# A hybrid attention and convolution block on one core: TensorE's order written by hand, and a value projection with weights stationary

## The chip, the cores and the metric

The kernel runs on one core of a Trainium2 chip. The metric is the device time of one execution in microseconds (us); the median over several executions is given. One more execution was recorded by the hardware profiler, and every row below is from that one. TensorE (PE in the rows, PEld for its weight loads) multiplies, VectorE (DVE), ScalarE (ACT) and GpSimd (POOL) do the rest, and SyncE (SP) issues nearly all transfers.

## The reference

The input has 2048 rows of 1024 numbers, ahead of which stand 16 meta tokens. All is in f32.

```python
proj = x @ w_in                        # q, k, v, z_a, u_c, g_c, z_c, gate_a, gate_c
# attention, 16 heads of 64, keys before the query only:
#   A[t,s] = sigmoid(z_ts) * prod_{s<j<t} (1 - sigmoid(z_tj))
o   = stick_breaking_attention(heads(q), heads(k), heads(v))
y_a = (o * silu(z_a)) @ w_attn_out
u   = u_c * sigmoid(g_c)
c   = silu(layer_norm(causal_depthwise_conv(u, dw_w, dw_b)))      # 31 taps
y_c = (c * silu(z_c)) @ w_conv_out
h   = sigmoid(gate_a) * y_a + sigmoid(gate_c) * y_c
out = layer_norm(alpha * x + h @ w_out)
```

## The kernel before

The sequence is worked in two halves of 1024 rows. Each half has a phase A (`phase_a`: projections, attention, convolution) and a phase B (`phase_b`: the convolution's layer norm and both output branches); `phase_c` makes the output. The sums are held to f32 by splitting each operand into a high and a low part, so that a projection chunk is 24 matmuls (`mm3`, L153 to L155: high by high, low by high, high by low, for 8 slices of the 1024 inputs). Chunks are 512 columns wide, or 352, 352 and 336 where the 16 meta columns ride along (k and the convolution's u and g in the first half). Weights are fetched by `split_w`: in the first half as raw f32, whose high part ScalarE copies (L136) and whose low part GpSimd subtracts (L137); both are kept in DRAM for the second half. There are two buffers for each.

Phase A goes over 8 pairs of heads. Attention of a pair is a walk over blocks of 256 queries (m) and, for each, over blocks of 256 keys (j) from the diagonal down to 0; I call one such (m, j) a tick. There are 10 ticks in a pair of the first half and 26 in one of the second, 288 in all, of which 64 are on the diagonal and 64 are low (j = 0; they carry the meta tokens). A tick is: 8 score matmuls (L382), the sigmoid (ScalarE, L385 and L388), a scan along the keys (VectorE, L404), 8 transposes of the scanned tile into two banks of two (`aT`, L416), their copies to SBUF (L420 to L423) and the weighing (L435): for each of two blocks of 128 keys and each of two heads one matmul of 256 columns against 64 columns of `dv`, the differences of v along the keys. A record of the profile is one pass; an f32 matmul leaves two, so that the four weighings of a tick are eight records. Low ticks add 4 narrow transposes (L440), a copy and 2 weighings with the meta keys (L445).

v is projected for two pairs at once with x stationary (`proj_v`, L277 to L279, 256 columns wide), written to DRAM (`v_d`) and read twice, shifted by a row, so that VectorE can take the differences (`load_v`, L348 and L350; `vd` is the one for the diagonal). The convolution's 31 taps (L479, L482) run on VectorE at low priority, two pieces of 512 columns a tap. Gates (`gates`) are projections that nothing in phase A needs; some are made between the ticks, the others in phase B (`between`), while the convolution's norm (`conv_norm`: L538 to L572 on VectorE, ScalarE and GpSimd, with two column sums on TensorE, L542 and L553) is worked. The order of every engine's instructions, TensorE's too, is made by a scheduler from priorities (`tc.high_priority`, `background`) and its own notion of durations.

Of the kernel before, what the change touches and what calls it, by code (L numbers as in the profile page):

```python
# [12 lines left out]
F32 = mybir.dt.float32  # L13
# [6 lines left out]
P = 128  # L20
# [5 lines left out]
HD = 64  # L26
# [13 lines left out]
def tile_stickbreak_hybrid(ctx: ExitStack, tc: tile.TileContext, t, out: bass.AP):  # L40
# [15 lines left out]
    v_d = dram.tile([1 + META + SEQ, D], F32, name="v_d")  # L56
# [14 lines left out]
    tail = const.tile([P, KC, 32], F32, name="tail")[:, :, 0:TAPS - 1]  # L71

# [53 lines left out]
    def split_w(key, src, shape=(KC, P), pool=None, bufs=2):  # L126
# [10 lines left out]
        nc.gpsimd.tensor_tensor(wl, raw, wh.bitcast(F32), ALU.subtract)  # L137
# [11 lines left out]
    def mm3(ps, w, xh, xl, c0, n, wk=lambda a, k: a[:, k, :]):  # L149
        wh, wl = w  # L150
        for k in range(KC):
            xhk, xlk = xh[:, k, c0:c0 + n], xl[:, k, c0:c0 + n]
            nc.tensor.matmul(ps, wk(wh, k), xhk, start=(k == 0), stop=False)  # L153
            nc.tensor.matmul(ps, wk(wh, k), xlk, start=False, stop=False)  # L154
            nc.tensor.matmul(ps, wk(wl, k), xhk, start=False, stop=(k == KC - 1))  # L155
# [18 lines left out]
    def alloc_x():  # L174
        xh = xp.tile([P, KC, XW], F32R, tag="xh", name="xh")
        xl = xp.tile([P, KC, XW], F32R, tag="xl", name="xl")
        return xh, xl
# [66 lines left out]
    def phase_a(hf, xh, xl, gate_items, order):  # L244
# [7 lines left out]
        with tc.tile_pool(name=f"pa{hf}", bufs=1) as pa:  # L252
            d1 = pa.tile([P, FW], F32, name="d1")
            nc.gpsimd.memset(d1, 0.0)
            if hf == 0:
                nc.sync.dma_start(out=v_d[0:1, :], in_=d1[0:1, 0:D])
            vms = [pa.tile([P, P], F32, name=f"vm{i}") for i in range(2)]
            ams = [pa.tile([P, 512], F32, name=f"am{i}") for i in range(2 - hf)]
            for x in vms + ams:
                nc.gpsimd.memset(x, 0.0)  # L260

            own = [slice(h * HD, (h + 1) * HD) for h in range(2)]
            oth = own[::-1]

            def proj_v(g):
                wv = w_in[:, :, 2 * D + g * 256:2 * D + (g + 1) * 256]
                w0 = split_w(("v", g, 0), wv[:, 0:4, :], (4, 256))
                w1 = split_w(("v", g, 1), wv[:, 4:8, :], (4, 256))
                tiles = [(i * P, P, META + hf * HALF + i * P) for i in range(8)]
                if hf == 0:  # L270
                    tiles.insert(0, (HALF, META, 0))
                for (c0, rows_, pos) in tiles:
                    ps = bank("mm", 2)[0:rows_, 0:256]
                    for k in range(KC):
                        wh, wl = (w0, w1)[k // 4]
                        a, b = xh[:, k, c0:c0 + rows_], xl[:, k, c0:c0 + rows_]
# [3 lines left out]
                    vs = pa.tile([P, 256], F32, tag="vs", name="vs", bufs=3 - hf)  # L280
                    nc.scalar.copy(vs[0:rows_], ps)
                    nc.sync.dma_start(out=v_d[1 + pos:1 + pos + rows_, g * 256:(g + 1) * 256], in_=vs[0:rows_])

            def proj_k(p):
                w = w_chunk(1, p)
                ka = [pa.tile([P, 32 + HALF], F32R, tag=f"ka{h}", name=f"ka{h}", bufs=2 - hf)[:, KM:] for h in range(2)]
                ks = ka
                if hf == 1:
                    ks = [pa.tile([P, HALF], F32R, tag=f"kb{h}", name=f"kb{h}", bufs=2) for h in range(2)]
# [422 lines left out]
```

## Time and profile before

| | |
|---|---|
| median of 3 runs | 3440.3 us (3435.89 to 3443.79) |
| profiled execution | 3442.93 us, span of its instructions 3441.1 us |
| busy: PE, PEld, DVE, ACT, POOL | 3303.5, 2602.1, 2159.5, 1150.9, 591.5 us |
| first score, last weighing of the first half | 171 and 1123 us |
| first score, last weighing of the second half | 1565 and 2970 us |

A busy time is the sum over an engine's instructions; a matmul's own length is longer than the distance from its start to the next one's, because matmuls overlap. What a matmul costs its engine is therefore read as the distance between two starts in the timeline.

### The profile page before, as it was taken

Reading aid. Unit: us, or ns where it says so; the run is one execution under the profiler, and the core shown is the slowest. Engines: PE = TensorE matmul, PEld = TensorE weight load, DVE = VectorE, ACT = ScalarE, POOL = GpSimd, SP = SyncE. Lnnn points to the kernel's source line nnn. Section 1 sums busy time; section 2 is a strip of 40 time slices with the busy share of each in tenths; the row PEclk is TensorE's granted clock in tenths of the full one; section 3 lists DMA queues with packets and bytes.
Section 4 is the critical chain, followed back from the end, with each engine's and each line's share of the span. In section 5 each row is a group of like instructions: output and inputs, shape, how many; then the busy total and the mean of one; then the engine's idle time right before and its main releaser. Section 6 shows DMA issues by size and latency. Waiting matters only on the chain.

```text
span 3441.1 us, 48095 instructions
## 1 busy us (share of the span) xinstructions
PE 3303.5 (96%) x18657; PEld 2602.1 (76%) x18657; DVE 2159.5 (63%) x2843; ACT 1150.9 (33%) x2284; POOL 591.5 (17%) x651
## 2 busy tenths in 40 slices
PE   7999999999999898999999999999999999999999
PEld 6987877877877676787777777777777777778777
DVE  6158578568569688216757685778567875364266
ACT  4243333333333243103443344334433434331100
POOL 2121312312312445100010001000100010122000
PEclk9999999999999998999999999999999999999999
DMA  8422522522523679762222222232212221567763
GB/s 291 148 98 96 187 99 100 190 92 106 186 93 119 220 265 320 284 203 75 73 72 76 101 72 72 65 100 70 87 59 94 77 83 67 167 232 249 249 205 104
DMA packets 302214, 476.86 MB, mean 139 GB/s; under 512 B 19354, under 2 KB 190962, under 8 KB 301986
## 3 DMA queue, kind: packets, MB, share of 16 engines
q1 hardware_dynamic: 299682, 465.26, 39.8%
q0 software_dynamic: 2304, 8.52, 0.8%
q8 instruction: 147, 2.41, 0.3%
q14 instruction: 81, 0.66, 0.1%
HBM read 297.35 MB, written 176.36 MB: 138 GB/s over the span
## 4 chain that ended last, share of the span: by engine, by line
PE 61%; DVE 6%; DMA 3%; issue 2%; POOL 1%; ACT 0%; SPq 0%; POOLq 0%; DVEq 0%; ACTq 0%
PE ps_o L435 9%; PE ps_mm L155 8%; PE ps_mm L153 8%; PE ps_mm L154 8%; PE ps_aT L416 7%; PE ps_z L382 6%; PE ps_mm L599 2%; PE ps_mm L597 2%; PE ps_mm L598 2%; DVE acc L482 2%; DVE f L404 1%; PE ps_mm L279 1%; PE ps_mm L278 1%; PE ps_mm L277 1%; DMA wl<-kept_in 1%
## 5 line engine op out<-in xcount | busy, mean ns | idle before, releaser
L153 PE MATMUL ps_mm<-xh,wh 128*128 128x512 f32 (+3 forms) x2336 | 872.0, 373 | 44.7 <-DVE ka L297 14.8
L404 DVE TENSOR_TENSOR_SCAN f<-f,d 128x1028 f32<-128x1028 f32 (+1 forms) x288 | 670.4, 2328 | 372.9 <-POOL f L389 159.8
L155 PE MATMUL ps_mm<-xh,wl 128*128 128x512 f32 (+3 forms) x2336 | 870.3, 373 | 13.8 <-POOL wl L137 12.4
L154 PE MATMUL ps_mm<-xl,wh 128*128 128x512 f32 (+3 forms) x2336 | 870.3, 373 | 0.0
L482 DVE SCALAR_TENSOR_TENSOR acc<-u,dww,acc 128x512 f32<-128x512 f32 x960 | 725.5, 797 | 6.6
L153 PEld LDWEIGHTS ps_mm<-xh,wh 128*128 128x128 f32 x2336 | 446.7, 191 | 121.7 <-issue 23.2
L155 PEld LDWEIGHTS ps_mm<-xh,wl 128*128 128x128 f32 x2336 | 445.1, 191 | 84.0 <-POOL wl L137 13.6
L154 PEld LDWEIGHTS ps_mm<-xl,wh 128*128 128x128 f32 x2336 | 446.4, 191 | 62.9 <-issue 2.0
L423 ACT COPY at<-ps_aT 128x512 f32<-128x512 f32 x448 | 260.3, 589 | 686.1 <-PE ps_aT L416 674.9
L435 PE MATMUL ps_o<-at,vp 128*64 128x256 f32 (+1 forms) x2048 | 408.2, 383 | 0.0
L416 PE MATMUL ps_aT<-ident,f 128*128 128x128 f32 x2176 | 349.9, 284 | 17.1 <-DVE f L404 16.9
L416 PEld LDWEIGHTS ps_aT<-ident,f 128*128 128x128 f32 x2176 | 237.3, 141 | 170.4 <-issue 147.0
L137 POOL TENSOR_TENSOR wl<-raw,wh 128x1024 fp32r<-128x1024 f32 x88 | 255.6, 2907 | 419.0 <-ACT wh L136 401.0
L382 PE MATMUL ps_z<-ka,q 128*128 128x256 f32 (+1 forms) x1664 | 290.2, 297 | 0.0
L388 ACT ACTIVATE f<-ps_z 128x512 f32<-128x512 f32 x448 | 253.1, 603 | 110.8 <-PE ps_z L382 101.4
L435 PEld LDWEIGHTS ps_o<-at,vp 128*64 128x64 f32 x2048 | 164.9, 136 | 138.2 <-issue 74.1
L389 POOL MEMSET f<- 128x4 f32 x288 | 30.2, 106 | 1371.5 <-ACT f L388 904.7
L382 PEld LDWEIGHTS ps_z<-ka,q 128*128 128x128 f32 x1664 | 232.5, 190 | 6.4 <-issue 2.4
L597 PE MATMUL ps_mm<-ah,wh 128*128 128x512 f32 x512 | 204.5, 400 | 8.6 <-DMA wh<-kept_w_attn_out 2.9
L598 PE MATMUL ps_mm<-al,wh 128*128 128x512 f32 x512 | 203.8, 398 | 7.3 <-DVE al L585 7.2
L599 PE MATMUL ps_mm<-ah,wl 128*128 128x512 f32 x512 | 205.0, 400 | 4.5 <-DMA wl<-kept_w_conv_out 2.9
L277 PE MATMUL ps_mm<-wh,xh 128*128 128x256 f32 (+1 forms) x544 | 156.6, 288 | 1.8 <-DMA wh<-kept_v 1.6
(147 smaller groups left out, 3653.5 us busy)
## 6 DMA issues: line engine op xcount, KB each, us to landing
wh<-kept_in SPq DMA_DIRECT2D x80, 512.0 KB, 3.6
wl<-kept_in SPq DMA_DIRECT2D x80, 512.0 KB, 4.4
raw<-w_in SPq DMA_DIRECT2D x72, 512.0 KB, 4.8
kept_in<-wh SPq DMA_DIRECT2D x64, 512.0 KB, 2.6
kept_in<-wl SPq DMA_DIRECT2D x64, 512.0 KB, 3.1
vp<-v_d SPq DMA_DIRECT2D x24, 512.0 KB, 4.2
vc<-v_d SPq DMA_DIRECT2D x24, 512.0 KB, 5.7
wh<-kept_w_conv_out SPq DMA_DIRECT2D x24, 512.0 KB, 3.6
```

The source lines that it names most:

```text
L153: nc.tensor.matmul(ps, wk(wh, k), xhk, start=(k == 0), stop=False)
L154: nc.tensor.matmul(ps, wk(wh, k), xlk, start=False, stop=False)
L155: nc.tensor.matmul(ps, wk(wl, k), xhk, start=False, stop=(k == KC - 1))
L382: nc.tensor.matmul(z[:, z0:z0 + nk], qs[h][s][:, tk], kp[h][:, ks0:ks0 + nk], start=(s == 0), stop=(s == 1))
L404: nc.vector.tensor_tensor_scan(ff, ff, dd, 0.0, ALU.mult, ALU.add)
L416: nc.tensor.transpose(tp[:, (2 * blk + q) * P:(2 * blk + q + 1) * P], f[:, 2 * h + q, c:c + P], ident)
L423: nc.scalar.copy(a, tp)
L435: nc.tensor.matmul(o_ps[hs, c:c + n], v[:, b8, hs], aT[h][:, a0 + c:a0 + c + n], start=(diag and blk == 0 and i == 0), stop=False)
L482: nc.vector.scalar_tensor_tensor(a, u[:, x + k:x + k + w], dww[:, i, k:k + 1], a, ALU.mult, ALU.add)
L597: nc.tensor.matmul(ps, wh[:, k, :], hi[k], start=(k == 0), stop=False)
L598: nc.tensor.matmul(ps, wh[:, k, :], lo[k], start=False, stop=False)
L599: nc.tensor.matmul(ps, wl[:, k, :], hi[k], start=False, stop=(k == KC - 1))
```

## The change

TensorE's order within phase A is no longer the scheduler's (`tc.manual_schedule`): the code's order holds. Each tick is the transposes of tick i, the scores of tick i + 2, at least 3000 columns of projection matmuls (`fill`), the weighing of tick i in one piece, and then the rest of the tick's share of projections. Projections are `Job`s in a written list; a job loads its own weights and those of the next one. v becomes such a job (`job_v`, weights stationary, 352, 352 and 336 or 512 columns wide): it leaves v with the keys along the columns, VectorE subtracts neighbouring columns (`dT`), and a `Turn` transposes the result, 8 blocks and in the first half one for the meta keys. `load_v`, its transfers and `vd` go; the last v of each block of queries is added when the output is taken (`og`). The meta part of a low tick has one transpose instead of four, and 4 narrow weighings in the same piece as the others. The low part of the weights is subtracted on VectorE (L139). In phase A there are 15 gates in each half instead of 8, so that phase B has 3 and 7 left to put between instead of 10 and 14. The convolutions of the first half run one pair earlier.

```diff
         raw = wp.tile([P, *shape], F32, tag="raw", name="raw")
         nc.sync.dma_start(out=raw, in_=src)
         nc.scalar.copy(wh, raw)
-        nc.gpsimd.tensor_tensor(wl, raw, wh.bitcast(F32), ALU.subtract)
+        nc.vector.tensor_tensor(wl, raw, wh.bitcast(F32), ALU.subtract)
...
-    def mm3(ps, w, xh, xl, c0, n, wk=lambda a, k: a[:, k, :]):
+    def mm3_steps(ps, w, xh, xl, c0, n):
...
         for k in range(KC):
             xhk, xlk = xh[:, k, c0:c0 + n], xl[:, k, c0:c0 + n]
-            nc.tensor.matmul(ps, wk(wh, k), xhk, start=(k == 0), stop=False)
-            nc.tensor.matmul(ps, wk(wh, k), xlk, start=False, stop=False)
...
+            nc.tensor.matmul(ps, wh[:, k, :], xhk, start=(k == 0), stop=False)
+            nc.tensor.matmul(ps, wh[:, k, :], xlk, start=False, stop=False)
+            nc.tensor.matmul(ps, wl[:, k, :], xhk, start=False, stop=(k == KC - 1))
+            yield 3 * n
...
+        with tc.tile_pool(name=f"pa{hf}", bufs=1) as pa, tc.manual_schedule(engines={mybir.EngineType.PE}):
...
-            def proj_v(g):
-                wv = w_in[:, :, 2 * D + g * 256:2 * D + (g + 1) * 256]
-                w0 = split_w(("v", g, 0), wv[:, 0:4, :], (4, 256))
...
-                        nc.tensor.matmul(ps, a, wh[:, k % 4, :], start=(k == 0), stop=False)
-                        nc.tensor.matmul(ps, b, wh[:, k % 4, :], start=False, stop=False)
-                        nc.tensor.matmul(ps, a, wl[:, k % 4, :], start=False, stop=(k == KC - 1))
...
+                def steps(self):
+                    st = self.begin() if self.begin else None
+                    for (c, n, parts) in self.chunks:
+                        ps = bank("mm", 2)[:, 0:n]
+                        for cost in mm3_steps(ps, self.w, xh, xl, c, n):
+                            yield cost
+                        self.evac(st, ps, c, n, parts)
...
+                def steps(self):
+                    dT = pairs[self.p]["dT"]
+                    dv = pa.tile([P, 8, P], F32, tag="dv1", name="dv1", bufs=2 - hf)
+                    for e in range(2):
+                        tp = bank("mm", 2)
+                        for b in range(4):
+                            c = VO + (4 * e + b) * P
+                            nc.tensor.transpose(tp[:, b * P:(b + 1) * P], dT[:, c:c + P], ident)
+                        yield 4 * 240
+                        nc.scalar.copy(dv[:, 4 * e:4 * e + 4, :], tp.rearrange("p (b c) -> p b c", c=P))
+                    pairs[self.p]["dv"] = [dv]
+                    if hf == 0:
+                        nc.sync.dma_start(out=dv_d[self.p], in_=dv)
+                        tp = bank("mm", 2)
+                        nc.tensor.transpose(tp[0:META, 0:P], dT[:, VO - META:VO], ident)
+                        yield 240
+                        vm = vms[self.p % 2]
...
...
+                def evac(vT, ps, c, n, parts):
+                    for (p0, l, d0) in parts:
...
+                    dT = pa.tile([P, VO + HALF], F32, tag="dT", name="dT", bufs=1)
+                    a = VO - off
+                    nc.vector.tensor_tensor(dT[:, a:], vT[:, a - 1:VO + HALF - 1], vT[:, a:], ALU.subtract)
+                    pairs[p]["dT"], pairs[p]["vL"] = dT, vL
+                return Job(2, p, kchunks, begin, evac)
...
-                    nc.vector.tensor_tensor(prev, prev, cur_, ALU.subtract)
-                    if e == hf:
-                        nc.vector.scalar_tensor_tensor(cur_, cur_, ident[:, P - 1:P], prev, ALU.mult, ALU.add)
-                        vd = cur_
...
+            def turn_meta(fm):
+                tp = bank("aT", 2)
+                nc.tensor.transpose(tp[:, 0:P], fm, ident)
+                a = pa.tile([P, P], F32, tag="am", name="am", bufs=2)
+                nc.scalar.copy(a, tp[:, 0:P])
+                return a
...
+            def weigh(p, i, aT, am):
...
+                for blk in range(2):
+                    b8 = 2 * (j % 4) + blk
+                    c = blk * P if j == m else 0
+                    for h in range(2):
+                        nc.tensor.matmul(o_ps[own[h], c:256], dv[:, b8, own[h]],
+                                         aT[h][:, blk * 256 + c:blk * 256 + 256],
+                                         start=(j == m and blk == 0), stop=False)
+                if j > 0:
+                    return
+                vm = pairs[p]["vm"]
+                for q in range(2):
+                    for h in range(2):
+                        nc.tensor.matmul(o_ps[own[h], q * P:(q + 1) * P], vm[:, 2 * h + q, :], am,
+                                         start=False, stop=(q == 1))
...
+                og = pa.tile([P, 256], F32, tag="og", name="og", bufs=2)
...
+                    g0 = (b % 4) * P
+                    qs = slice(q * P, (q + 1) * P)
+                    nc.vector.scalar_tensor_tensor(og[:, qs], o_ps[:, qs], pairs[p]["vL"][:, b:b + 1], z[:, g0:g0 + P],
+                                                   ALU.add, ALU.mult)
...
+            prep = [job_k(0), job_q(0, 0), job_v(0), job_z(0), Turn(0, 0), job_q(0, 1)] + jobs_conv(0)
+            body, rest = [], []
+            for p in range(NPAIR):
+                a, b, n = [], [], p + 1
+                if hf == 1 and p > 0:
+                    a.append(job_q(p, 1))
+                if n < NPAIR:
+                    cv = jobs_conv(n)
+                    if hf == 0:
+                        a += [job_k(n), job_v(n), job_q(n, 0, last0 - 1), cv[0], Turn(n, 0), cv[1], job_z(n)]
+                        b += [job_q(n, 1, T - 2)] + take(1)
+                    else:
+                        a += [job_v(n), job_k(n)] + cv + [job_z(n), job_q(n, 0, last0 - 1), Turn(n, lasthi + 1)]
+                        b += take(1)
+                else:
+                    a += take(7 if hf == 0 else 6)
+                    b += take(1 if hf == 0 else 2)
+                body.append(a)
+                rest.append(b)
...
+            def run(job):
+                job.load()
+                nxt = [x for x in flat[pos[id(job)] + 1:] if isinstance(x, Job)][:1]
+                for x in nxt:
+                    x.load()
+                yield from job.steps()
...
-                                for q in range(2):
-                                    if diag and blk > q:
...
-                                    parts = [(vd, blk * P, P)] + ([(dv[j // 4], P, P)] if blk == 0 else [])
-                                else:
-                                    parts = [(dv[j // 4], 0, 256)]
-                                for i, (v, c, n) in enumerate(parts):
-                                    nc.tensor.matmul(o_ps[hs, c:c + n], v[:, b8, hs], aT[h][:, a0 + c:a0 + c + n],
-                                                     start=(diag and blk == 0 and i == 0), stop=False)
...
-                            tp = bank("aT", 2)
-                            for s in range(4):
-                                nc.tensor.transpose(tp[0:META, s * P:(s + 1) * P], f[:, s, 0:META], ident)
...
-                                hs = slice(h * HD, (h + 1) * HD)
-                                nc.tensor.matmul(o_ps[hs], vm[:, hs], a[:, h * 256:(h + 1) * 256],
-                                                 start=False, stop=True)
-                    g0 = (m % 2) * 256
-                    og = pa.tile([P, 256], F32, tag="og", name="og", bufs=2 - hf)
-                    nc.vector.tensor_tensor(og, o_ps, za[ci][:, g0:g0 + 256], ALU.mult)
...
+            feed.finish(0)
+            score_all(0, 1)
+            feed = Feed(prep[4:])
+            feed.finish(0)
             for p in range(NPAIR):
-                vt, ks, za = cur["v"], cur["k"], cur["z"]
-                with tc.high_priority(HIGH):
-                    attention(p, 0, ks, cur["0"], vt, za)
-                    attention(p, 1, ks, cur["1"], vt, za)
-                for ch in order[1 + p % (len(order) - 1)]:
-                    job(ch, p + 1)
-            while convs:
-                job("c", NPAIR)
-            return items
...
+                fa, fb = Feed(body[p]), Feed(rest[p])
+                for i in range(T):
+                    fd, n = (fa, T - 2 - i) if i < T - 2 else (fb, T - i)
+                    quota = fd.left // n
+                    before = fd.left
+                    with tc.high_priority(HIGH):
+                        (aT, fm), am = turn(p, i), None
+                    p2, i2 = (p, i + 2) if i + 2 < T else (p + 1, i + 2 - T)
+                    if p2 < NPAIR:
+                        with tc.high_priority(HIGH):
+                            sc = scores(p2, i2)
+                            next(sc)
+                        if ticks[i2][1] == 0:
+                            fd.fill(1536, i)
+                            with tc.high_priority(HIGH):
+                                next(sc)
+                    if ticks[i][1] == 0:
+                        with tc.high_priority(HIGH):
+                            am = turn_meta(fm)
+                    fd.fill(3000, i)
+                    with tc.high_priority(HIGH):
+                        weigh(p, i, aT, am)
+                    live.pop((p, i - 1), None)
+                    fd.fill(quota - (before - fd.left), i)
+                    if n == 1:
+                        fd.finish(i)
+            return gq
```

TensorE in a plain tick of the second half, before: `ps_o` is the output of the weighing, `vp` the differences of v, `ps_aT` the transposes' bank.

```order
L154 MATMUL ps_mm<-xl,wh 128x512
L435 MATMUL ps_o<-at,vp_17597 64x256 x3
L416 MATMUL ps_aT<-ident,f 128x128 x4
L435 MATMUL ps_o<-at,vp_17592 64x256
L416 MATMUL ps_aT<-ident,f 128x128 x4
L382 MATMUL ps_z<-ka_17528,q_17956 128x272
L382 MATMUL ps_z<-ka_17528,q_17957 128x272
L382 MATMUL ps_z<-ka_17529,q_17958 128x272
```

The weighing stands in two pieces of three and one instructions, with four transposes between them.

The same place with the change (`dv0` are now the differences, numbers behind names tell buffers apart; the first row is the last of the eight score matmuls):

```order
L474 MATMUL ps_z_17077<-ka1_15062,q111_16273 128x272
L156 MATMUL ps_mm_16994<-xh_11729,wh_16781 128x512
L157 MATMUL ps_mm_16994<-xl_11730,wh_16781 128x512
L158 MATMUL ps_mm_16994<-xh_11729,wl_16782 128x512
L156 MATMUL ps_mm_17090<-xh_11729,wh_16781 128x512
L157 MATMUL ps_mm_17090<-xl_11730,wh_16781 128x512
L158 MATMUL ps_mm_17090<-xh_11729,wl_16782 128x512
L547 MATMUL ps_o_16890<-at_17052,dv0_16232 64x256
L547 MATMUL ps_o_16890<-at_17059,dv0_16232 64x256
L547 MATMUL ps_o_16890<-at_17052,dv0_16232 64x256
L547 MATMUL ps_o_16890<-at_17059,dv0_16232 64x256
```

All four weighings stand together, with six projection matmuls between the scores and them; the transposes that stood between the two pieces are now ahead of the scores.

VectorE in a pair of the first half, before, from the first tap of a convolution (`acc`) on; `q` and `sg` are evacuations of projections, `f` a scan:

```order
L479 TENSOR_SCALAR acc<-u,dww,vec 128x512 x2
L482 SCALAR_TENSOR_TENSOR acc<-u,dww,acc 128x512 x10
L449 TENSOR_TENSOR og<-ps_o,za 128x256
L482 SCALAR_TENSOR_TENSOR acc<-u,dww,acc 128x512 x5
L320 TENSOR_TENSOR q_9483<-ps_mm,q_9482 64x512
L320 TENSOR_TENSOR q_9485<-ps_mm,q_9484 64x512
L482 SCALAR_TENSOR_TENSOR acc<-u,dww,acc 128x512 x3
L221 TENSOR_TENSOR sg<-ps_mm,sg 128x512
L482 SCALAR_TENSOR_TENSOR acc<-u,dww,acc 128x512 x10
L221 TENSOR_TENSOR sg<-ps_mm,sg 128x512
L482 SCALAR_TENSOR_TENSOR acc<-u,dww,acc 128x512 x4
```

The same stretch with the change:

```order
L498 MEMSET d_1154 128x4
L489 MEMSET d_1154 128x4
L443 SCALAR_TENSOR_TENSOR acc<-u,dww,acc 128x512 x3
L139 TENSOR_TENSOR wl<-raw,wh 128x1024
L443 SCALAR_TENSOR_TENSOR acc<-u,dww,acc 128x512 x2
L390 TENSOR_TENSOR q_8374<-ps_mm,q_8373 64x512
L390 TENSOR_TENSOR q_8376<-ps_mm,q_8375 64x512
L443 SCALAR_TENSOR_TENSOR acc<-u,dww,acc 128x512 x4
L563 SCALAR_TENSOR_TENSOR og<-ps_o,vL,za 128x128 x2
L443 SCALAR_TENSOR_TENSOR acc<-u,dww,acc 128x512 x2
L228 TENSOR_TENSOR sg<-ps_mm,sg 128x512
```

The subtraction of the weights (L139) stands in VectorE's queue between taps, ahead of an evacuation of q.

## Rows read from the trace of the kernel before

**Rows 1.** Stages: window, length, busy time of each engine, PEclk, DMA share, GB/s.

```profile
171.00:1123.00 952.00, 902.72 (x5594) 751.59 (x5592) 667.82 (x863) 337.21 (x727) 228.55 (x207) 0.98 0.37 124
1123.00:1565.00 442.00, 398.27 (x1762) 320.80 (x1763) 226.42 (x315) 109.91 (x168) 148.82 (x80) 0.95 0.74 256
1565.00:2970.00 1405.00, 1402.38 (x8305) 1026.44 (x8303) 954.61 (x1133) 560.92 (x1160) 115.89 (x291) 1.00 0.23 77
```

**Rows 2.** TensorE's waits, 171 to 1123 us: total, times, longest.

```profile
PE ps_aT L416 <- DVE f L404: 16.9, 12, 3.6
PE ps_mm L153 <- DVE ka L297: 14.8, 6, 3.8
```

**Rows 3.** Timeline of TensorE, a tick of the second half: start, length, line.

```profile
2019.38 0.39 PE L153 MATMUL ps_mm<-xh,wh 128*128 128x512 f32 x1
2019.61 0.40 PE L154 MATMUL ps_mm<-xl,wh 128*128 128x512 f32 x1
2019.94 1.08 PE L435 MATMUL ps_o<-at,vp 128*64 128x256 f32 x6
2020.94 0.66 PE L416 MATMUL ps_aT<-ident,f 128*128 128x128 f32 x4
2021.36 0.36 PE L382 MATMUL ps_z<-ka,q 128*128 128x256 f32 x1
2021.65 0.65 PE L435 MATMUL ps_o<-at,vp 128*64 128x256 f32 x2
2022.23 0.44 PE L416 MATMUL ps_aT<-ident,f 128*128 128x128 f32 x2
```

**Rows 4.** Timeline of TensorE, a tick whose weighing stands in one piece.

```profile
1944.30 1.08 PE L435 MATMUL ps_o<-at,vp 128*64 128x256 f32 x8
1945.31 1.09 PE L416 MATMUL ps_aT<-ident,f 128*128 128x128 f32 x8
```

**Rows 5.** Timeline of TensorE, the meta tokens' weighing of the last low tick.

```profile
1122.32 0.65 PE L445 MATMUL ps_o<-am,vm 128*64 128x256 f32 x4
1122.90 0.50 PE L153 MATMUL ps_mm<-xh,wh 128*128 128x512 f32 x1
1123.24 0.39 PE L154 MATMUL ps_mm<-xl,wh 128*128 128x512 f32 x1
```

**Rows 6.** Groups of VectorE by line and shape, 171 to 1123 us.

```profile
L482 DVE SCALAR_TENSOR_TENSOR acc<-u,dww,acc 128x512 f32<-128x512 f32 x436 | 342.9, 842 | 0.5
L404 DVE TENSOR_TENSOR_SCAN f<-f,d 128x1028 f32<-128x1028 f32 x48 | 109.9, 2290 | 19.9 <-POOL f L389 11.6 <-POOL f L392 8.1
...
L401 DVE COPY d<-f 128x4 f32<-128x4 f32 x48 | 19.0, 397 | 0.4
...
L348 DVE TENSOR_TENSOR vp<-vp,vc 128x1024 f32<-128x1024 f32 x6 | 7.4, 1226 | 5.8 <-DMA vc<-v_d 5.7
```

**Rows 7.** The same groups of VectorE, 1565 to 2970 us.

```profile
L482 DVE SCALAR_TENSOR_TENSOR acc<-u,dww,acc 128x512 f32<-128x512 f32 x480 | 351.8, 757 | 6.1
```

**Rows 8.** Groups of GpSimd by line, 171 to 1123 us.

```profile
L137 POOL TENSOR_TENSOR wl<-raw,wh 128x1024 fp32r<-128x1024 f32 x51 | 147.3, 2890 | 244.1 <-ACT wh L136 235.4 <-DVE acc L482 8.5
```

**Rows 9.** Groups of ScalarE by line, 1565 to 2970 us.

```profile
L423 ACT COPY at<-ps_aT 128x512 f32<-128x512 f32 x352 | 205.3, 588 | 530.0 <-PE ps_aT L416 527.6 <-PE ps_z L382 0.9 <-PE ps_o L435 0.7
L388 ACT ACTIVATE f<-ps_z 128x512 f32<-128x512 f32 x352 | 198.8, 604 | 40.8 <-PE ps_z L382 33.9 <-PE ps_aT L440 6.9
```

**Rows 10.** Timeline of TensorE in phase B of the first half.

```profile
1186.55 0.67 PE L542 MATMUL ps_z<-cs,ones 128*128 128x512 f32 x1
...
1264.22 0.39 PE L597 MATMUL ps_mm<-ah,wh 128*128 128x512 f32 x1
```

**Rows 11.** Timeline of TensorE in phase B of the second half.

```profile
2987.63 0.59 PE L542 MATMUL ps_z<-cs,ones 128*128 128x512 f32 x1
```

**Rows 12.** Timeline of VectorE, the same stretch.

```profile
3027.39 0.69 DVE L585 TENSOR_TENSOR al<-d,ah 128x512 fp32r<-128x512 f32 x1
...
3053.86 0.68 DVE L585 TENSOR_TENSOR al<-d,ah 128x512 fp32r<-128x512 f32 x1
```

More of the change, by code (lines that the diff above doesn't have):

```diff
@@ L255, in phase_a @@
             if hf == 0:
[L256 to L260, printed above, removed]
+                vms = [pa.tile([P, 4, HD], F32, name=f"vm{i}") for i in range(2)]
+                for x in vms:
+                    nc.gpsimd.memset(x, 0.0)
             own = [slice(h * HD, (h + 1) * HD) for h in range(2)]
@@ L284, in proj_k @@
[L284 to L289, printed above, removed]
-                for (c, n, parts) in kchunks:
-                    ps = bank("mm", 2)[:, 0:n]
-                    mm3(ps, w, xh, xl, c, n)
+            pairs = [{} for _ in range(NPAIR)]
@@ new lines, in phase_a, with __init__, load @@
+            class Job:
+                def __init__(self, seg, i, chunks, begin, evac, first=0):
+                    self.seg, self.i, self.chunks, self.begin, self.evac, self.first = seg, i, chunks, begin, evac, first
+                    self.cost = 3 * KC * sum(n for _, n, _ in chunks)
+                    self.w = None
+                def load(self):
+                    if self.w is None:
+                        self.w = w_chunk(self.seg, self.i)
+                def steps(self):
[5 more added lines that the diff above has]
+                        self.evac(st, ps, c, n, parts)
@@ new lines, in phase_a, with __init__, load @@
+            class Turn:
+                def __init__(self, p, first):
+                    self.p, self.first, self.cost = p, first, 9 * 240
+                def load(self):
+                    pass
+                def steps(self):
[15 more added lines that the diff above has]
+                        vm = vms[self.p % 2]
+                        for s in range(4):
+                            nc.scalar.copy(vm[32 * s:32 * s + META, s, :], tp[0:META, own[s // 2]])
+                        pairs[self.p]["vm"] = vm
+                        nc.sync.dma_start(out=vm_d[self.p], in_=vm)
@@ new lines, in job_k, with begin, evac @@
+            def job_k(p):
+                def begin():
+                    ka = [pa.tile([P, 32 + HALF], F32R, tag=f"ka{h}", name=f"ka{h}", bufs=2)[:, KM:] for h in range(2)]
+                    ks = ka
+                    if hf == 1:
+                        for h in range(2):
+                            nc.gpsimd.dma_start(out=ka[h], in_=k_d[p, h])
+                        ks = [pa.tile([P, HALF], F32R, tag=f"kb{h}", name=f"kb{h}", bufs=2) for h in range(2)]
+                    pairs[p]["k"] = (ka, ks)
+                    return ks
+                def evac(ks, ps, c, n, parts):
@@ L509, in phase_a @@
[L509 to L521 removed]
+                    pairs[p].setdefault("z", []).append(z)
```

421 lines of the change are left out of this document (220 added, 201 removed).

## The prediction

> **What bounds the kernel now.** I read the stages first. In the second half's phase A TensorE is busy 1402.38 of 1405 us at a granted clock of 1.00, VectorE 954.61 (68%) and ScalarE 560.92 (40%) [rows 1]: there whatever TensorE no longer has to do comes off the time, as long as VectorE and ScalarE keep up. In the first half's phase A TensorE is busy 902.72 of 952 us [rows 1]; its longest waits are for VectorE, 16.9 us for scans and 14.8 us for evacuations of k [rows 2], though VectorE is busy only 70% of the stage: it is late in some stretches, not in all. The stage between has 44 us without TensorE [rows 1]. So two questions decide: what TensorE's work costs after the change, and whether VectorE and the chain of phase B then end later than it.
>
> **TensorE's work.** Durations of matmuls are distances between starts.
>
> Weighing. Plain matmuls of 512 columns follow each other in 0.23 us (2019.38 to 2019.61); the one ahead of a weighing takes 0.33, so going into a weighing costs 0.10 [rows 3]. In a split tick the first piece takes 1.00 us (six records), the second 0.58 (two) [rows 3]; a whole weighing of eight records takes 1.01 [rows 4]. A split tick pays 0.57 for the second piece and 0.10 for going in again: 0.67. The trace has 217 such second pieces of two records (2021.65 is one), and the change leaves none: 217 x 0.67 = -145 us. What coming out costs I leave equal: 0.34 instead of 0.23 for the first 512 columns after a weighing [rows 5], once per tick now, against two exits into transposes.
>
> Meta keys. A separate meta weighing takes 0.58 us, 0.10 in and 0.11 out [rows 5], 0.79 in all. In one piece with the others it is half the columns of a weighing, so half of 1.01 [rows 4]. Saved: 0.29 x 64 = -18 us (estimate; between 0.21 and 0.35 each, -13 to -22). Four transposes take 0.42 us (2020.94 to 2021.36) [rows 3], 0.105 each, so 192 fewer are -20 us. The 136 new ones for v's differences are +14.
>
> v. By 0.231 us for 512 columns a matmul costs 0.116 for 256, 0.159 for 352, 0.152 for 336. Before: 1632 of 256 columns, 189 us. After: 8 pairs x 24 x 0.470 in the first half, 90, and 8 x 48 x 0.231 in the second, 89. Together -10 us. On the diagonal the same columns are weighed in fewer matmuls; I take 0 (bounds -10 and +5).
>
> Sum: -145 - 18 - 20 + 14 - 10 = -179 us; with the bounds -165 to -195. The gates, convolutions and projections that move are the same matmuls elsewhere.
>
> **VectorE in the first half.** The subtraction on GpSimd took 2.89 us 51 times in this stage [rows 8]. The nearest row on VectorE, a subtraction of the same 128x1024, is 1.23 us [rows 6], so it gets 51 x 1.23 = 63 us more. Against it, a tap takes 842 ns in this stage [rows 6] and 757 in the second half, where GpSimd doesn't subtract weights [rows 7]: 436 x 0.085 = 37 us that come back, less what GpSimd's other work costs. With the shifted v's reads and subtractions gone as well, I take VectorE's load as unchanged.
>
> The page "SBUF — State Buffer" of the Trainium skill, section "Who interferes with whom", says that GpSimd and VectorE lock a port pair against each other for a whole instruction. By it up to 51 x 2.89 = 147 us of VectorE would come back, and the rival "waits vanish" below would be the case; the sum would be 3224. The rows give a quarter of that on the taps, and I go by them.
>
> But TensorE's part shrinks. Between the last piece of u and k's third chunk of the next pair, TensorE has five 512-column chunks (24 x 0.231 = 5.5 us each), three of k (11.3 us) and five ticks of about 3 us: 54 us. VectorE has in the same place 62 taps at 0.757 (47 us; some overlap, so 41 to 47), five scans at 2.29 [rows 6] (11.5), four weight subtractions (4.9) and the evacuations (about 5): 62 to 68, say 65. The two banks of the projections let an evacuation be late by one chunk, 4 us. So TensorE loses about 65 - 54 - 4 = 7 us a pair, 50 us over seven pairs, and some 10 more at scans and at v's differences: 60 us, against 67 now: the 49 without TensorE [rows 1], and an estimated 18 that don't show as idle, because a matmul's row is 0.40 us long and the next starts after 0.23 [rows 3], so that each of some 100 waits hides its first 0.17. Net -7. Bounds: -47 (nearly all cover found) and +83 (taps at 842 ns, and weights late by another 5 us a pair).
>
> **Second half.** Per tick TensorE keeps about 6 us; ScalarE's two copies (0.588 each) and two sigmoids (0.604) [rows 9] make 2.4 us of it, VectorE's share rises from 68% to 73%. Between the transposes and the weighing of one tick stand eight scores (0.95) and six projections (1.39), 2.3 us, against 1.2 for the two copies. A fixed order can't step around a late copy, so I add 10 us over 208 ticks (bounds 0 and 40).
>
> **Phase B of the first half.** From the first column sum to the first branch matmul go 77.7 us [rows 10], all but some waits filled by gates. After the change 63 gate matmuls (14.6 us) and the next half's first transposes (2.5) stand behind that sum. In the second half, where GpSimd subtracts no weights, the same chain takes 39.8 us to the first low part of the branch's input and 66.2 to the last [rows 11, 12]. The first branch chunks (11 us) can't end before the last of them: 66 - 14.6 - 2.5 - 11 = 38 us of idle TensorE. Of the stage's 44 us I take half as lying ahead of the branches and going: +16 (bounds -15 and +40). In the second half 7 gates remain, 78 us, and cover the 66: 0.
>
> **Sum.** -179 - 7 + 10 + 16 = -160 us on the profiled 3442.9 (span 3441.1 and 1.8 around it): 3282.9. That execution was 2.6 above the median, so 3280 us.
>
> **Rivals.** (1) Waits vanish: with GpSimd out of VectorE's way the first half's waits shrink to 20 us and the chain of phase B is as short as in the second half. 3280 - 40 - 16 = 3224. For it: VectorE's 70%. Against: taps, not averages, stand ahead of the evacuations. (2) VectorE is the bound in the first half: taps stay at 842 ns and the weights' low parts queue behind them; +83 in place of -7 gives 3370. For it: every low part now stands behind taps in a queue that runs in order. (3) Phase B's chain stays at 77.7 us with fewer gates over it: idle 60 in place of 38, 3302. (4) Slower: the hand order waits at each weighing, because ScalarE's copies stand behind sigmoids and evacuations. If a copy ends 0.56 us behind the 2.3 us of cover in each of 288 ticks, the 160 us are gone; at 0.65 us it is 3280 + 187 = 3467. That takes copies that end 2.9 us after the transposes: two copies, two sigmoids and another evacuation in a row (about 3.0), in every tick. ScalarE at 40% speaks against it.
>
> **How the numbers follow.** Forecast 0.54, rival 1 0.20, rival 2 0.12, rival 3 0.07, rival 4 0.07. The range 3210 to 3350 holds the forecast, rivals 1 and 3. A measurement here tells about 0.2% (7 us) from no change; within that only the edge of rival 4 lies (0.02). Faster 0.93, same 0.02, slower 0.05.
>
> **What would show it.** Weighings in runs of eight or twelve records; the second half's phase A near 1300 us with TensorE still at 99%; in the first half waits of projections for VectorE's evacuations of k, q or for low parts of weights, 60 us in all; a gap of some 40 us ahead of the first branch matmul. I am wrong if TensorE waits for ScalarE's copies at the weighings, if the first half waits over 100 us, or if a weighing in one piece isn't 0.67 us cheaper.

## The result and the profile after

The changed kernel takes 3350.6 us (median of 4, 3348.7 to 3352.3), the kernel before 3442.0 in the same comparison: a ratio of 0.974 (95% interval 0.972 to 0.975). It is faster, by 91 us where I forecast 160, and 0.6 us above the range.

The stages of the profiled execution (span 3349.6 us), cut at the same places as [rows 1]: first score, last weighing of the first half, first score and last weighing of the second. Columns as there.

```profile
139.80:1147.60 1007.80, 963.13 (x5836) 826.29 (x5834) 713.77 (x991) 358.28 (x851) 82.07 (x170) 0.98 0.39 131
1147.60:1496.30 348.70, 292.42 (x1210) 229.44 (x1208) 184.00 (x281) 94.83 (x140) 73.64 (x55) 0.91 0.76 264
1496.30:2887.60 1391.30, 1337.83 (x8143) 1029.51 (x8141) 944.19 (x1147) 554.22 (x1211) 89.70 (x296) 0.98 0.21 71
```

Against before, the five stages that these cuts make changed by -31 us (up to the first score), +56, -93, -14 and -9. In the first half the work that moved explains it. Phase B has 552 passes fewer (x1210, before x1762 [rows 1]): 336 are the seven gates (78 us at 11.1 each), 72 are z and a part of q of the next half, which now stand behind its first score (17 us), 144 are v. In the second half it does not. This is the last stage, in the kernel before and then in the changed one:

```profile
2970.00:3441.00 471.00, 455.90 (x1962) 366.77 (x1960) 237.87 (x403) 83.56 (x129) 65.38 (x46) 0.99 0.63 214
2887.60:3349.60 462.00, 444.67 (x1928) 361.52 (x1922) 237.26 (x404) 81.87 (x127) 63.83 (x46) 0.99 0.63 215
```

It lost 34 passes (8 us), where seven gates are 336: the scheduler had drawn most of them ahead of the last weighing already in the kernel before, whatever their place in the code. So by these moves the second half's phase A got some 25 us of work, 8 of gates and 17 of z and q.

The stage that missed is the second half's phase A: 1391 us, of which TensorE is without work for 53 us, at a granted clock of 0.98, where before it was busy 1402.38 of 1405 us at 1.00. Its longest waits, and under them the longest of the first half (total, times, longest):

```profile
PE ps_z L474 <- POOL q L392: 27.4, 8, 5.3
PE ps_mm L314 <- ACT dv L316: 18.3, 7, 2.7
PE ps_o L547 <- ACT at L523: 3.0, 2, 2.5
PE ps_o L547 <- DVE d L493: 2.9, 2, 2.2
```

```profile
PE ps_mm L156 <- DVE ka L371: 19.6, 6, 3.3
```

The weighing itself became what I had costed. TensorE in a tick of the second half:

```profile
2093.51 0.39 PE L157 MATMUL ps_mm<-xl,wh 128*128 128x512 f32 x1
2093.74 0.40 PE L158 MATMUL ps_mm<-xh,wl 128*128 128x512 f32 x1
2094.07 1.08 PE L547 MATMUL ps_o<-at,dv 128*64 128x256 f32 x8
2095.08 0.50 PE L156 MATMUL ps_mm<-xh,wh 128*128 128x512 f32 x1
```

One run of eight records, 1.01 us from start to start (2094.07 to 2095.08), entered for 0.33 after a distance of 0.23 between the projections ahead of it.

What the 27.4 us are is seen in a stretch of all engines at the end of a pair (start, length, engine; in brackets the idle time before, and what ended it):

```profile
1849.25 2.35 ACT L388 CAST q<-ps_mm 64x512 fp32r<-64x512 f32 x4 [0.30 <-PE ps_mm L158]
...
1851.62 0.58 ACT L316 COPY dv<-ps_mm 128x512 f32<-128x512 f32 x1
...
1851.92 3.42 DVE L443 SCALAR_TENSOR_TENSOR acc<-u,dww,acc 128x512 f32<-128x512 f32 x5
...
1852.26 0.66 PE L314 MATMUL ps_mm<-ident,dT 128*128 128x128 f32 x4 [2.62 <-ACT dv L316]
...
1854.71 0.36 PE L474 MATMUL ps_z<-kb,q 128*128 128x256 f32 x1
1855.23 2.45 DVE L496 TENSOR_TENSOR_SCAN f<-f,d 128x1092 f32<-128x1092 f32 x1
1857.57 1.42 DVE L443 SCALAR_TENSOR_TENSOR acc<-u,dww,acc 128x512 f32<-128x512 f32 x2
...
1858.88 1.42 DVE L390 TENSOR_TENSOR q<-ps_mm,q 64x512 fp32r<-64x512 f32 x2
1859.70 1.27 POOL L392 CAST q<-q 64x512 fp32r<-64x512 f32 x2 [10.36 <-DVE q L390]
...
1860.36 1.86 PE L474 MATMUL ps_z<-kb,q 128*128 128x256 f32 x7 [5.29 <-POOL q L392]
...
1862.02 0.63 PE L156 MATMUL ps_mm<-xh,wh 128*128 128x512 f32 x1
...
1862.45 0.63 PE L157 MATMUL ps_mm<-xl,wh 128*128 128x512 f32 x1
```

The next pair's first q ends at 1849. ScalarE casts its four parts, and only then the first half of v's transposed differences (1851.62), for whose bank TensorE waits 2.6 us. The scores of the next pair start at 1854.71 and need q's low part. VectorE makes it at 1858.88, behind five taps, a scan and two taps; GpSimd's copy follows, and TensorE waits until 1860.36. Then it starts at the lower of its two clocks, 1.2 GHz in place of 2.4 (0.43 us from 1862.02 to 1862.45); the granted clock (PEclk) around it:

```profile
1853.00:1861.00 8.00, 2.71 (x20) 0.77 0.33 123
1861.00:1866.00 5.00, 5.00 (x22) 0.68 0.00 0
1866.00:1870.00 4.00, 4.00 (x21) 1.00 0.02 4
```

### The profile page after: what moved, and what is told of

It reads as the page before. It is cut to its first block, busy times and chain, and to the rows that moved or that the text cites. A ratio compares the mean times of both kernels' runs of the same rounds, so it can differ in the third digit from the quotient of the medians.

```text
span 3349.6 us, 46178 instructions
## 1 busy us (share of the span) xinstructions
PE 3150.1 (94%) x17929; PEld 2555.2 (76%) x17929; DVE 2148.9 (64%) x2955; ACT 1143.3 (34%) x2418; POOL 312.9 (9%) x582
## 4 chain that ended last, share of the span: by engine, by line
PE 59%; DVE 25%; DMA 6%; issue 5%; ACT 2%; POOL 2%; SPq 1%; DVEq 0%; POOLq 0%; ACTq 0%
DVE acc L443 13%; PE ps_mm L156 12%; PE ps_mm L157 10%; PE ps_mm L158 10%; PE ps_o L547 6%; PE ps_z L474 6%; DVE f L496 5%; PE ps_aT L516 5%; PE ps_mm L749 2%; PE ps_mm L747 2%; PE ps_mm L748 2%; DVE wl L139 1%; DMA zc<-zc_d 1%; DMA bx<-x 1%; PE ps_o L555 1%
## 5 line engine op out<-in xcount | busy, mean ns | idle before, releaser
L156 PE MATMUL ps_mm<-xh,wh 128*128 128x512 f32 (+3 forms) x2656 | 1013.4, 382 | 47.1 <-DVE ka L371 19.6
L157 PE MATMUL ps_mm<-xl,wh 128*128 128x512 f32 (+3 forms) x2656 | 974.4, 367 | 2.4 <-DVE xl L210 2.4
L158 PE MATMUL ps_mm<-xh,wl 128*128 128x512 f32 (+3 forms) x2656 | 974.0, 367 | 0.0
L156 PEld LDWEIGHTS ps_mm<-xh,wh 128*128 128x128 f32 x2656 | 504.8, 190 | 192.8 <-issue 102.9
L158 PEld LDWEIGHTS ps_mm<-xh,wl 128*128 128x128 f32 x2656 | 503.9, 190 | 74.4 <-issue 0.5
L157 PEld LDWEIGHTS ps_mm<-xl,wh 128*128 128x128 f32 x2656 | 505.4, 190 | 53.0 <-DVE xl L210 2.7
L523 ACT COPY at<-ps_aT 128x512 f32<-128x512 f32 x448 | 241.2, 590 | 459.5 <-PE ps_aT L516 458.7
L547 PE MATMUL ps_o<-at,dv 128*64 128x256 f32 (+1 forms) x2304 | 307.3, 387 | 5.9 <-ACT at L523 3.0
L547 PEld LDWEIGHTS ps_o<-at,dv 128*64 128x64 f32 x2304 | 142.8, 138 | 148.6 <-issue 98.4
L139 DVE TENSOR_TENSOR wl<-raw,wh 128x1024 fp32r<-128x1024 f32 x88 | 110.4, 1256 | 144.0 <-ACT wh L138 134.6
L138 ACT CAST wh<-raw 128x1024 fp32r<-128x1024 f32 x88 | 92.1, 1049 | 287.9 <-PE ps_mm L157 248.0
```

Of the source, the lines that this page charges most:

```text
L156: nc.tensor.matmul(ps, wh[:, k, :], xhk, start=(k == 0), stop=False)
L157: nc.tensor.matmul(ps, wh[:, k, :], xlk, start=False, stop=False)
L158: nc.tensor.matmul(ps, wl[:, k, :], xhk, start=False, stop=(k == KC - 1))
L547: nc.tensor.matmul(o_ps[own[h], c:256], dv[:, b8, own[h]], aT[h][:, blk * 256 + c:blk * 256 + 256], start=(j == m and blk == 0), stop=False)
```

## The experiments

In each diff the lines are those of the changed kernel, if nothing else is said. The kernel before took 3442.0 us beside the changed kernel, and 3437.0, 3445.6 and 3441.6 beside the runs below; a difference of a few us between two of them may be none.

**q made earlier.** In the second half:

```diff
-    a += [job_v(n), job_k(n)] + cv + [job_z(n), job_q(n, 0, last0 - 1), Turn(n, lasthi + 1)]
+    a += [job_v(n), job_k(n)] + cv + [job_q(n, 0, last0 - 1), job_z(n), Turn(n, lasthi + 1)]
```

> The changed kernel (3350.6 us), with one edit: in the second half the next pair's first q projection stands ahead of z's two chunks instead of behind them. Theory (q is made too late: about 5.7 us before the first scores that need it, and its low part waits behind taps and a scan in VectorE's queue): the waits of scores for GpSimd's copy of q (27.4 us) and of v's transposes for ScalarE (18.3 us) go, and with them the stretches at half clock behind them; the second half's phase A falls from 1391 to about 1320 us, the time to 3280 (3265 to 3295). Rival (the hand order has too little slack at the end of a pair whatever stands there): the wait moves to z, to v's transposes or to the scans, and the time stays within 15 us of 3350.

3316.0 us, 35 less than 3350.6; the second half's phase A went from 1391 to 1359. The wait for GpSimd's q is gone and the one for `dv` fell from 18.3 to 5.2, so the theory holds for these; but of the 40.5 us that the two lost, 24 came back as other waits, most of them at the weighing (20.4 for 3.0), the rest for scans:

```profile
PE ps_o L547 <- ACT at L523: 20.4, 8, 2.9
PE ps_aT L516 <- DVE f L496: 6.5, 7, 1.8
PE ps_mm L314 <- ACT dv L316: 5.2, 7, 0.8
```

```profile
2012.13 2.42 DVE L496 TENSOR_TENSOR_SCAN f<-f,d 128x1092 f32<-128x1092 f32 x1
...
2014.59 0.30 ACT L508 COPY fm<-f 128x128 f32<-128x128 f32 x1 [5.77 <-DVE f L496]
2014.79 1.07 ACT L523 COPY at<-ps_aT 128x512 f32<-128x512 f32 x2
...
2015.42 1.56 PE L547 MATMUL ps_o<-at,dv 128*64 128x256 f32 x8 [2.85 <-ACT at L523]
```

ScalarE's copy of the meta keys' part (L508) stands ahead of the copies for a weighing (L523) and waits for a late scan; the weighing waits with them.

**Fewer taps.**

```diff
-    for k in range(1, TAPS):
+    for k in range(1, 9):
```

> The changed kernel with 9 of the convolution's 31 taps; 22 are left out, so that the convolution isn't the reference's. Theory (evacuations and q's low parts are late because taps stand ahead of them in VectorE's queue): in the first half the waits for k (19.6 us) go, in the second those for GpSimd's copy of q (27.4 us) fall below 5; both phases A get 25 to 50 us shorter each, the time is 3255 to 3300. Rival (ScalarE's four casts, VectorE's subtraction and GpSimd's copy, 5.1 us in a row, are too long for the 5.7 us that the order leaves): the wait for q stays above 15 us, the time above 3310.

3256.3 us with 9 of the 31 taps. The waits for k fell from 19.6 to 2.0 us, the one for q is gone, and `dv`, which only ScalarE delays, is as it was (18.4). The stages:

```profile
141.70:1106.90 965.20, 946.18 (x5836) 813.81 (x5834) 466.42 (x639) 358.20 (x851) 70.05 (x170) 1.00 0.41 137
1458.70:2796.90 1338.20, 1318.07 (x8141) 1018.91 (x8141) 708.69 (x795) 554.64 (x1211) 86.70 (x296) 0.99 0.21 74
```

Phase A is 43 us shorter in the first half and 53 in the second. So the taps on VectorE, which is busy only 71% and 68% of these stages with all of them, make TensorE wait, directly or through GpSimd. Whether by their place in the queue or by their load, this run can't tell, as it takes away both; the runs that only move jobs can.

**The subtraction of the weights back on GpSimd,** and, in the kernel before, that move alone:

```diff
-    nc.vector.tensor_tensor(wl, raw, wh.bitcast(F32), ALU.subtract)
+    nc.gpsimd.tensor_tensor(wl, raw, wh.bitcast(F32), ALU.subtract)
```

> The changed kernel, with the subtraction of the weights' low part back on GpSimd. Theory by the rows of taps (what VectorE gives and gets cancels): within 12 us of 3350. Rival (a port lock for a whole instruction: 59 subtractions of 2.9 us each cost VectorE their full length in the first half's phase A, where evacuations are already late): slower by 40 to 100 us.

> The kernel before (3440 us) with the weights' low part subtracted on VectorE, nothing else. If a subtraction on GpSimd holds VectorE up for nearly its length, as putting it back into the changed kernel showed (56 us), the same move is worth much of that here: 3385 to 3420. If the price there was special to the hand order, whose evacuations were late already: within 12 us of 3440.

Back on GpSimd: 3406.6 us, 56 more. Alone in the kernel before: 3388.8 us, 57 less than the 3445.6 of the kernel before beside it, a ratio of 0.984 (0.982 to 0.986). So this one line is worth some 55 us of the change's 91. Where it comes from, in the first half's phase A: VectorE's taps, scans, subtractions and v's differences in the changed kernel, then taps, scans and differences, GpSimd's subtractions and the stage with it back.

```profile
L443 DVE SCALAR_TENSOR_TENSOR acc<-u,dww,acc 128x512 f32<-128x512 f32 x480 | 352.6, 789 | 1.2
L496 DVE TENSOR_TENSOR_SCAN f<-f,d 128x1028 f32<-128x1028 f32 x48 | 110.3, 2297 | 57.1 <-POOL f L484 28.8 <-POOL f L481 28.3
...
L139 DVE TENSOR_TENSOR wl<-raw,wh 128x1024 fp32r<-128x1024 f32 x60 | 73.4, 1223 | 121.7 <-ACT wh L138 113.5 <-PE ps_aT L516 8.1
...
L351 DVE TENSOR_TENSOR dT<-vT 128x1040 f32<-128x1040 f32 x8 | 9.9, 1237 | 8.1 <-ACT vT L342 8.1
```

```profile
L443 DVE SCALAR_TENSOR_TENSOR acc<-u,dww,acc 128x512 f32<-128x512 f32 x480 | 396.0, 885 | 0.8
L496 DVE TENSOR_TENSOR_SCAN f<-f,d 128x1028 f32<-128x1028 f32 x48 | 124.2, 2587 | 138.3 <-POOL f L481 105.5 <-POOL f L484 32.8
...
L351 DVE TENSOR_TENSOR dT<-vT 128x1040 f32<-128x1040 f32 x8 | 21.3, 2664 | 42.4 <-ACT vT L342 42.4
```

```profile
L139 POOL TENSOR_TENSOR wl<-raw,wh 128x1024 fp32r<-128x1024 f32 x60 | 155.0, 2583 | 374.6 <-ACT wh L138 346.0 <-PE ps_z L474 28.6
```

```profile
139.90:1205.20 1065.30, 979.86 (x5834) 838.53 (x5833) 718.77 (x931) 359.06 (x851) 235.84 (x230) 0.97 0.36 124
```

Back on GpSimd, taps cost VectorE 43 us more (396.0 for 352.6), scans of this width 14 (2587 ns for 2297) and v's differences 11, and it is spared 73: its busy time stays nearly as it was (718.77 us for 713.77), and the stage still gets 58 us longer. TensorE's waits for k grow from 19.6 to 38.0 us, those for the gates' evacuations (`sg`) from 3.8 to 20.7. In the kernel before it is the same the other way round:

```profile
171.40:1072.60 901.20, 886.72 (x5606) 742.57 (x5604) 657.21 (x910) 336.74 (x729) 74.32 (x155) 1.00 0.39 130
```

VectorE is busy 657 us, before 668 [rows 1]; the stage is 51 us shorter, TensorE's waits fell from 49 us to 15 and its clock rose from 0.98 to 1.00. So the average load, by which I had set the move at nothing, was right and says nothing; what TensorE pays for is each evacuation that is late. The page "SBUF — State Buffer" of the Trainium skill ("Who interferes with whom") has the two engines lock each other out for whole instructions, VectorE's with two inputs in SBUF among them, as the taps, scans and differences here. The direction agrees: against GpSimd's 155 us VectorE lost some 70 on the rows above, while evacuations of q, which read PSUM, kept their time (686 ns for 687); but so did the scans of 1092 columns (2422 for 2430). How much of the 55 us is that and how much is that the low parts come sooner (1.22 in place of 2.58 us) was not separated.

**Gates left to phase B.** Of the first half's last pair:

```diff
-    a += take(7 if hf == 0 else 6)
+    a += take(3 if hf == 0 else 6)
```

> The changed kernel, with three gates instead of seven made among the last pair's ticks of the first half; four gates (44 us of TensorE) are left to phase B, ahead of its branches. Theory (TensorE's gaps of 13.8, 5.8 and 7.1 us ahead of the first branch matmul are the norm's chain without cover): the gaps go, phase A of the first half gets 44 us shorter, and the time falls by 25 to 35 us, to 3315 to 3325. Rival (the last pair's ticks now lack cover for scans and copies, or the gaps belong to the next half's build): faster by less than 10 us.

3305.3 us, 45 less: more than I expected. Four gates are 44 us of TensorE:

```profile
140.10:1099.80 959.70, 917.23 (x5644) 789.65 (x5642) 709.27 (x987) 349.98 (x839) 76.50 (x170) 0.99 0.38 129
1099.80:1454.50 354.70, 328.13 (x1402) 260.65 (x1400) 193.84 (x285) 97.53 (x148) 75.98 (x55) 0.97 0.81 283
```

Phase A is 48 us shorter and phase B only 6 longer, with 36 us more of TensorE's work in it. In the changed kernel the norm's chain was open for about that long: its stage has 56 us without TensorE, here 27, and the granted clock rises from 0.91 to 0.97. The longest open stretch in the changed kernel, from the second column sum to the first branch matmul (TensorE alone):

```profile
1184.30:1215.00 30.70, 5.35 (x20) 0.57 0.53 188
```

**The weighing in two pieces again.**

```diff
                         nc.tensor.matmul(o_ps[own[h], c:256], dv[:, b8, own[h]],
...
+                    if blk == 0:
+                        yield
...
-                        weigh(p, i, aT, am)
+                        wg = weigh(p, i, aT, am)
+                        next(wg)
+                    fd.fill(1, i)
+                    with tc.high_priority(HIGH):
+                        for _ in wg:
+                            pass
```

> The changed kernel, with three projection matmuls put between the two halves of each weighing, so that TensorE goes into and out of weighings twice per tick. Theory of the prediction (a piece of four records takes 0.58 us, a whole one 1.01, going in costs 0.10 and coming out 0.11): 0.36 us more in each of some 285 ticks, 100 us, so 3450 (3425 to 3470); the second half's phase A alone 208 x 0.36 = 75 us longer. Rival (the price of pieces is hidden by the next weight loads): under 30 us more.

3400.1 us, 50 more: between the two. The price of a piece is as forecast:

```profile
2103.73 0.40 PE L158 MATMUL ps_mm<-xh,wl 128*128 128x512 f32 x1
2104.06 0.65 PE L547 MATMUL ps_o<-at,dv 128*64 128x256 f32 x4
2104.64 0.51 PE L156 MATMUL ps_mm<-xh,wh 128*128 128x512 f32 x1
2104.98 0.40 PE L157 MATMUL ps_mm<-xl,wh 128*128 128x512 f32 x1
```

0.33 in, 0.58 for four records, 0.34 out. But the second half's phase A grew by 38 us in place of 75: the waits for q fell from 27.4 to 9.8 us, and the half clock behind them with them. So TensorE's extra work was done in part, it seems, while it would have waited.

**The order given back to the scheduler.**

```diff
-        with tc.tile_pool(name=f"pa{hf}", bufs=1) as pa, tc.manual_schedule(engines={mybir.EngineType.PE}):
+        with tc.tile_pool(name=f"pa{hf}", bufs=1) as pa:
```

> The changed kernel without the one switch that keeps TensorE's order in phase A as written: the scheduler orders it again, and splits the weighings again (564 runs of weighings in place of 289). Theory (the written order saves some 145 us of pieces and pays about 100 of them back in waits): 3380 to 3410, which is the kernel before with its subtraction on VectorE (3389), less 40 for the meta keys, plus 40 for the gates that phase B lacks. Rival (the written order's waits cost as much as its pieces save): 3340 to 3360, or less.

3356.2 us: the written order is worth 5.6 us (0.17%), no more than a measurement can tell. The theory fell and the rival's time came out. Phase A, phase B and the second half's phase A:

```profile
133.70:1089.70 956.00, 943.04 (x5656) 792.88 (x5656) 704.25 (x989) 359.39 (x840) 81.70 (x172) 1.00 0.38 130
1089.70:1448.10 358.40, 335.18 (x1412) 265.65 (x1411) 192.60 (x285) 101.79 (x152) 77.04 (x55) 0.96 0.82 285
1448.10:2886.30 1438.20, 1435.79 (x8151) 1046.61 (x8149) 935.85 (x1147) 572.72 (x1211) 101.94 (x296) 1.00 0.20 68
```

With the weighings split again, the second half is 47 us longer than with the written order, though TensorE idles 2 us of it in place of 53: there the whole weighings gain more than the waits cost. The first half's phase A is 52 us shorter, but mostly because less work stands in it: 180 passes fewer than in the changed kernel (x5656, x5836), some 44 us, and phase B has 202 more (x1412, x1210) and is only 10 us longer, as TensorE idles 23 us in it in place of 56. That is the edit of the four gates, made by the scheduler: with it the written order's phase A takes 960 us, the scheduler's 956. So what the written order loses in the first half is for the most part the place of the gates.

**The list mended.** First the two edits that gained alone, then also the copy of the meta keys' part on GpSimd, then v ahead of k in the first half, then two gates more for phase B (the last edit is shown against the run before it):

```diff
-    nc.scalar.copy(fm.rearrange("p (s c) -> p s c", s=4), f[:, :, 0:32])
+    nc.gpsimd.tensor_copy(fm.rearrange("p (s c) -> p s c", s=4), f[:, :, 0:32])
...
-    a += [job_k(n), job_v(n), job_q(n, 0, last0 - 1), cv[0], Turn(n, 0), cv[1], job_z(n)]
+    a += [job_v(n), job_k(n), job_q(n, 0, last0 - 1), cv[0], Turn(n, 0), cv[1], job_z(n)]
...
-    a += take(3 if hf == 0 else 6)
+    a += take(1 if hf == 0 else 6)
```

> The changed kernel with both edits that gained alone: q ahead of z in the second half (-35 us) and four gates more left to the first half's phase B (-45 us). They touch different stages, so they add: 3270 (3263 to 3280). If one of them only moved the other's wait: above 3290.

3272.7 us: they add.

> As the one with q first and four gates more for phase B, and the copy of the meta keys' part (fm) made by GpSimd instead of ScalarE. Theory (what is left in the second half is ScalarE's queue: the copies for a weighing, ready, stand behind the copy of fm, which waits 5.8 us for a late scan): the weighings' waits of 20.4 us go, with the half clock behind them 25 us in all: 3245. Rival (the scan itself is late, and the next transposes wait for it instead): less than 8 us.

3256.6 us, 16 less where the theory gave 25: the weighings' waits for copies fell from 20.8 to 2 us, but in their place come 7.9 us for the output's evacuation, `og`.

> As the one with q first, four gates more for phase B and GpSimd's copy (3256.6 us), and v ahead of k in the first half. v leaves by ScalarE, k partly by VectorE, so k's evacuation comes some 11 us of TensorE later against the taps. Theory (VectorE's taps, scans and evacuations between u and k's third chunk, 65 us, are 7 us more than TensorE's work and one chunk of cover): with 11 us more cover the waits for k (19.7 us) go, 3230 to 3240. Rival (the next evacuation by VectorE, q's, waits instead): within 8 us of 3256.

3231.2 us, 25 less, in the range that the theory gave: the waits for k fell from 19.7 to 7.9 us, not to nothing, and the first half's clock rose from 0.99 to 1.00. VectorE's busy time is as before (706.68 us; 709.62 in the run before it).

```profile
139.40:1068.90 929.50, 903.75 (x5644) 777.75 (x5642) 706.68 (x987) 340.69 (x807) 95.54 (x202) 1.00 0.39 133
1068.90:1425.50 356.60, 327.82 (x1401) 260.46 (x1399) 192.55 (x285) 99.94 (x150) 74.08 (x55) 0.98 0.81 282
```

> As the one with v first, and two gates more (22 us of TensorE) left to the first half's phase B, nine in all. Theory (the gaps left there, some 17 us ahead of the next half's transposes, are still the norm's chain and the build without cover): 10 to 18 us faster than that one. Rival (the last pair's ten ticks have by now less to put between their scans and weighings): no faster, or slower.

3229.7 us, within the spread of the one before, where the theory gave 10 to 18 less: phase A gets 18 us shorter, but phase B 13 longer and the stage up to the first score 4. So the rival holds, and two more gates gave nothing. These last two are the fastest, at 0.9385 of the time before (0.937 to 0.940). None of these edits was run with the order given back to the scheduler, so how much of the last 121 us needs the written order is not shown.

## Why the prediction was wrong

- **TensorE's work** was right in its prices: 1.01 us for a whole weighing, 0.58 for a piece, 0.10 in and 0.11 out, in the changed kernel and in the one split again. It was wrong to book 179 us as time. It is time only where TensorE is always busy, and in the split kernel the pieces cost half of their price. Without the subtraction's line the change gave 35 us (3406.6), and the written order, against the scheduler's order of the same kernel, 5.6.
- **The second half** is the step that failed: "A fixed order can't step around a late copy, so I add 10 us over 208 ticks (bounds 0 and 40)". It has 53 us of waits, and a clock of 0.98 for 1.00, 2% of 1391, is up to 28 more; together about 80 where I had 10. These 70 us are the size of the whole miss. (That the stage would be "near 1300 us" was low by some 25 besides, the work that moved into it.) TensorE was busy 96% of the stage, where I had written 99; none of my three signs of being wrong caught it. I had looked at the cover inside a tick, 2.3 us against 1.2 for the copies, and there the weighings wait 6 us in all. I had not followed the list of projections across the end of a pair, where q's last step and the scores that need it stand 5.7 us apart, with four casts, VectorE's queue and GpSimd's copy between them. The listings of the order ahead of the prediction show a tick and a stretch within a pair, not this place. Moving q by two chunks gave 35 us back.
- **The first half** came out near my 60 us (45 of waits, and a clock of 0.98), in part by the mechanism named: the waits for k are 19.6 us where I had booked 50, they go without the taps, and they shrink with 11 us more of TensorE's work ahead of them. That the number fits is luck, for two things cancel in it that I had not booked. Alone, the subtraction that I set at nothing takes 51 us off this stage in the kernel before, which leaves 15 us of waits and a clock of 1.00; with the rest of the change there are 45 and 0.98 again. Nor were there "some 100 waits" that hide 18 us before: the profile lists 32 in all, and the clock of 0.98 in [rows 1], which I had not read, is up to 19 us of that stage by itself.
- **Phase B** was right in size: TensorE idles 56 us in that stage, where I had 44 and 16 more; 25 of them lie between the second column sum and the first branch matmul, where I had put 38. The four gates confirm it.
- **Rivals.** None came as written. ScalarE's copies weren't late at every weighing; nor did the first half's waits vanish. VectorE was the main cause, but by the order of its queue, not by its load: moving q gave 35 us and moving v 25 with VectorE as busy as before (942.3 us for 944.2 in the one's stage, 706.7 for 709.6 in the other's). Rival 2's 3370 us is near the measured time, but the taps did not stay at 842 ns (789). The Trainium skill's rule of a locked port, which I had weighed lightly, points the way of the part that gained most; how much of that gain is its doing stays open.

## What to carry to other kernels

A written order on one engine is only as good as the other engines' queues, which still run in theirs: for each hand-over follow the whole chain (cast, subtraction, copy) and what stands ahead of each link in its queue, above all where one repetition passes into the next. An engine at 70% can still be what the bound engine waits for, so work moved onto or off it is priced by what it delays, not by its sum. And test each part of a change alone: here one line that looked like nothing gave more than half of the gain, and the written order gained next to nothing over the scheduler's until its list was put right.

## What the runs showed of the hardware that was not expected

A wait of 5.3 us, close behind one of 2.6, left TensorE at 1.2 GHz for a while: a mean granted clock of 0.68 over the next five us, with matmuls of 512 columns 0.43 us apart in place of 0.23. The first half's phase A ran at 0.98 with 45 us of waits, with v ahead of k at 1.00 with 26. So a wait costs more than its length here; the sums of waits above don't hold that part.
